# Bias tables copied within HBM and four temporaries of their own for six evictions in a transformer kernel on one Trainium2 core

## The chip, the core and the metric

The kernel runs on one core of one Trainium2 chip, as a single launch. The metric is the device time of one execution in microseconds. The times shown are those of three runs and of one execution that was taken with the hardware profiler. The engines are named as in the profile: PE (TensorE, with PEld for its weight loads), DVE (VectorE), ACT (ScalarE), POOL (GpSimd) and SP (SyncE, which here issues the weight DMAs).

## The reference

The input is one sequence of 512 tokens of width 1024 in float32. It goes through two layers of a first block and one layer of a second block. In outline (norms, gains and rotary embeddings are left out):

```
for l in 0, 1:
    x = x + 0.5 * swiglu(norm(x), ffn1_w_gu[l], ffn1_w_down[l])
    h = norm(x)
    parts of h @ w_in[l]:
        o_a = stick-breaking attention (4 heads)
        o_b = compressed + selected + windowed attention (8 heads, 2 key groups)
        o_c = attention over the 256 best keys by an indexer (4 heads)
    g_a, g_b, g_c = sigmoid(h @ w_gate[l])
    x = x + (g_a * (o_a @ w_br_a) + g_b * (o_b @ w_br_b) + g_c * (o_c @ w_br_c)) @ w_out
    x = x + 0.5 * swiglu(norm(x), ffn2_w_gu[l], ffn2_w_down[l])
second block:
    dilated attention in 3 groups of 8 heads, with a bias table per group and head,
    beside a gated convolution; then a swiglu FFN
```

The bias of the dilated attention depends on the distance of query and key and on the head alone: `bias_tab[rel_bucket(offset * dilation)]`.

## The kernel before

Activations lie transposed, 1024 channels in eight chunks of 128 partitions by 512 tokens. All weights come as one stream of 550 units of 128 x 1024 float32 (512 KB) in the order in which they are used. SP loads them into a ring of three staging buffers (`w_dma`, L133), ACT makes a rounded high part (L141) and DVE the rest (L142, `w_prep`), into a ring of five. A product is three matmuls, high x high, high x low and low x high (`mm3`, L172 to L174). The weights are prepared three units ahead of the unit in use.

The code is written as generators. A main generator yields after each product and holds the stream's matmuls; in the two mixers a side generator (`gen_side`: indexer, compression, attention) runs beside it. The side generator waits at named flags that the main one sets. A scheduler then orders the instructions of each engine by priority and by its own estimate of durations; each engine executes its list strictly in that order, waiting for what an instruction needs.

FFN front (`gen_ffn`): the norm's factor per token is not known when the first products run. The first two units, c = 0 and 1, are computed on unnormed input; then `stats_a` (L218, L223) and `rsqrt` (L205 to L210) make the factor, and `bcast` spreads it with a matmul (L231, L232, L233) into `rb`, which each eviction multiplies in (L261). The next units follow one by one up to c = 12.

Bias tables (`bias_rows`, L1005): in the very first FFN, after unit 2, three pairs of small matmuls (L1015) look up the bias rows of each group, DVE adds a mask (L1018), and POOL writes each group's 8 rows of 384 values 128 times into the HBM tensor `dr_b` (L1019), which the second block's attention reads much later (L1172), each partition from another offset:

```
t = self.f(o + 2328 + 384 * g, 384)[0:8]
nc.vector.tensor_tensor(t, ps[0:8, 0:384], cb[...], op=ALU.add)
nc.gpsimd.dma_start(self.dr_b[g], t[:, None, :].to_broadcast([8, 128, 384]))
```

Mixer front (`gen_mix`): after a first group for the indexer (`ev1`), the main generator computes two column blocks for the compressed keys and values (a "tunit" is one such block of eight products) and four for the stick-breaking queries and keys. Each is evicted from its PSUM bank by a multiplication with `rb` into a temporary (L470 in `ev_cmp`, L486 in `ev_sb`), which `split` (L179, L180, L182, L183) turns into two parts. There are two temporaries, in the region M_PT. The indexer (`gen_idx`) uses the same two as room for its transposed copies: `tpose_dup` copies to them (L592) and transposes them on PE (L595); its scores are L630, and DVE adds them up (L636). After the front the main generator goes on with the compression's first product (L500, L501), further column groups, 24 gate units (L522) and the first branch. M_NQ, 2048 values wide, later takes the queries of the sparse attention (`group(w["nq"])`).

The attention pairs of the side work are L777 (scores), L793 (transposes) and L801 (values).

Of the kernel before, what the change touches and what calls it, by code (L numbers as in the profile page):

```python
# [9 lines left out]
F32 = mybir.dt.float32  # L10
# [46 lines left out]
M_NQ = M_SV + 1024  # L57
M_SC = M_NQ + 2048
M_P = M_SC + 1152
M_PT = M_P + 2048  # L60
# [49 lines left out]
class Build:  # L110
# [133 lines left out]
    def gen_ffn(self, wgu, wdn, l, done, halves=None):  # L244
        nc = self.nc
        Y = A_Y
        gs = [self.f(Y + 1536 + 512 * i, 512) for i in range(2)]
        tt = [self.f(Y + 2560 + 512 * i, 512) for i in range(2)]
        rb = self.f(A_RB, 512)
        ring = tuple(range(8))  # L250

        def fs(c):
            o = R_O + (c % FSLOTS) * 1024
            return self.r(o, 512), self.r(o + 512, 512)

        def gkey(c, up, k):
            return (wgu, l, np.arange(128 * k, 128 * k + 128), np.arange(128) + 128 * c + up * DFF)

        def evac(c, pg, pu):
            i = c % 2  # L260
            nc.vector.tensor_tensor(gs[i], pg, rb, op=ALU.mult)  # L261
            nc.scalar.activation(gs[i], gs[i], AF.Silu)
            nc.vector.tensor_tensor(gs[i], pu, gs[i], op=ALU.mult)  # L263
            hi, lo = fs(c)
            self.split(hi, lo, gs[i])

        def up(cs):
            ps = {(c, up): self.bank(ring) for c in cs for up in (0, 1)}
            order = [(c, up, k) for c in cs for up in (0, 1) for k in range(8)]
            if len(cs) == 2:  # L270
                order.sort(key=lambda e: e[2])
            for c, up, k in order:
                self.mm3(ps[c, up], self.w(gkey(c, up, k)), self.h(k), k == 0, k == 7)
                yield
            if len(cs) == 2:
                pst = self.bank(ring)
                self.bcast(self.stats_a((self.acc,), pst), tt_flat, pst, rb)
            for c in cs:
                evac(c, ps[c, 0], ps[c, 1])
            if cs[0] == 2 and self.first:  # L280
                self.first = False
                self.bias_rows()

        tt_flat = self.f(Y + 2560, 512)

        def down(grp, cs):
            nk = len(cs)
            if grp == 0:
                order = [(m, j) for m in range(8) for j in range(nk)]
            else:  # L290
                order = [(m, j) for m in range(2) for j in range(nk - 1)] + [(m, nk - 1) for m in range(2)]
                order += [(m, j) for m in range(2, 6 if halves else 8) for j in range(nk)]
            ps = {}
            for m, j in order:
                if j == 0:
                    ps[m] = self.bank(ring)
                key = (wdn, l, np.arange(128) + 128 * cs[j], np.arange(128) + 128 * m)
                self.mm3(ps[m], self.w(key), fs(cs[j]), j == 0, j == nk - 1)
                yield
                if j == nk - 1:  # L300
                    done(grp, m, ps[m], tt[m % 2], rb)
            if grp == 0 or not halves:
                return

            tl = {}
            for i in range(2):
                sl = slice(256 * i, 256 * i + 256)
                for m in (6, 7):
                    ps = self.bank(ring)[:, sl]
                    for j in range(nk):  # L310
                        if i == 0:
                            tl[m, j] = self.w((wdn, l, np.arange(128) + 128 * cs[j], np.arange(128) + 128 * m))
                        self.mm3(ps, tl[m, j], [a[:, sl] for a in fs(cs[j])], j == 0, j == nk - 1)
                        yield
                    done(grp, m, ps, tt[m % 2][:, sl], rb, sl)
                halves(i)

        c0 = list(range(11))
        c1 = list(range(11, 22))
        for cs in [(0, 1)] + [(c,) for c in range(2, 13)]:  # L320
            yield from up(cs)
        yield from down(0, c0)
        for c in c1[2:]:
            yield from up((c,))
        yield from down(1, c1)
# [60 lines left out]
    def gen_mix(self, l):  # L386
        nc = self.nc
# [54 lines left out]
            with self.late(-5000):  # L442
                evac(ps)

        def tmp2(i, o=M_PT):
            return self.f(o + (i % 2) * 512, 512)

        def ev1(t, ps):
            for o, n, p in ((M_IQ + t * 288, 288, 0), (M_G1 + t * 160, 160, 288)):
                nc.scalar.activation(self.f(o, n), ps[:, p:p + n], AF.Copy, scale=rc[:, t:t + 1])  # L450
# [8 lines left out]
        def blk(kv, hl):  # L459
            return 1122 * (2 * kv + hl)  # L460
# [5 lines left out]

        def ev_cmp(kv):
            def evac(ps):
                t = tmp2(kv)
                nc.vector.tensor_tensor(t, ps, rb, op=ALU.mult)  # L470
                for g in range(2):
                    sl = slice(64 * g, 64 * g + 64)
                    o = 544 * g
                    self.split(stk[sl, blk(kv, 0) + o:blk(kv, 0) + o + 512],
                               stk[sl, blk(kv, 1) + o:blk(kv, 1) + o + 512], t[sl])
                b = stk[:, blk(kv, 0):blk(kv, 0) + 2244].rearrange("p (h n) -> p h n", h=2)
                nc.gpsimd.dma_start(b[64:128, :, 0:511], b[0:64, :, 1:512])
                nc.gpsimd.dma_start(b[0:64, :, 545:1057], b[64:128, :, 544:1056])
            return evac
# [2 lines left out]

        def ev_sb(i):
            def evac(ps):
                t = tmp2(i)
                nc.vector.tensor_tensor(t, ps, rb, op=ALU.mult)  # L486
                self.split(self.r(R_QK + i * 1024, 512), self.r(R_QK + i * 1024 + 512, 512), t,
                           scale=0.125 if i < 2 else None)
            return evac
# [3 lines left out]
        for kv in range(2):  # L493
            ps = self.bank(ring)
            o = ps[:, 0:192].rearrange("p (l g c) -> p l g c", l=2, c=32)
# [22 lines left out]
        for m in range(8):  # L518
            for br in range(3):
                def evac(ps):  # L520
                    t = tmp2(n, M_IQ)
                    nc.vector.tensor_tensor(t, ps, rb, op=ALU.mult)  # L522
                    nc.gpsimd.dma_start(self.dr_g[m, :, br * 512:br * 512 + 512], t)
                yield from tunit("w_gate", np.arange(128) + 1024 * br + 128 * m, evac)
                n += 1

        self.mt = self.h_tile(F32)
        for m in range(8):
            g = self.merged(m)
# [475 lines left out]
    def bias_rows(self):  # L1005

        nc = self.nc
        o = A_Y + 3584
        cb = self.f(o, 2304)[0:32]
        nc.scalar.dma_start(cb, self.ap["cb"])  # L1010
        tab = self.f(o + 2304, 24)[0:32]
        nc.scalar.dma_start(tab, self.ap["par"][2][0:32, 296:320])
        for g in range(3):
            ps = self.bank(tuple(range(8)))
            nc.tensor.matmul(ps[0:8, 0:384], lhsT=tab[:, 8 * g:8 * g + 8], rhs=cb[:, 384 * g:384 * g + 384],  # L1015
                             start=True, stop=True)
            t = self.f(o + 2328 + 384 * g, 384)[0:8]
            nc.vector.tensor_tensor(t, ps[0:8, 0:384], cb[0:8, 1152 + 384 * g:1536 + 384 * g], op=ALU.add)  # L1018
            nc.gpsimd.dma_start(self.dr_b[g], t[:, None, :].to_broadcast([8, 128, 384]))  # L1019

    def gen_mix2(self):
        nc = self.nc
# [402 lines left out]
    def run(self, upto=99, start=0):  # L1425
        tc, nc, ap = self.tc, self.nc, self.ap
        with tc.tile_pool(name="sb", bufs=1) as sb, tc.tile_pool(name="hp", bufs=1) as self.hp, \
# [9 lines left out]
            self.sqt = [self.f(A_Y + 512 + 512 * i, 512) for i in range(2)]  # L1437
            self.dr_x = dr.tile([128, 4096], F32, name="dr_x")
            self.dr_b = dr.tile([3, 8, 128, 384], F32, name="dr_b")
            self.dr_c = dr.tile([8, 128, 512], F32, name="dr_c")  # L1440
            self.dr_s = dr.tile([512, 12], F32, name="dr_s")
            self.m2 = {}
# [17 lines left out]
            for l in range(2 if start == 0 else 0):  # L1460
                g = par[:, 24 * l:24 * l + 24]
# [22 lines left out]
            o = M  # L1484
# [100 lines left out]
```

## Time and profile before

| | |
|---|---|
| median of 3 runs | 3531.94 us |
| the three runs | 3525.71, 3531.94, 3532.26 us |
| profiled execution, its own time | 3525.48 us |
| span of that execution, first to last instruction | 3523.7 us |
| mean granted TensorE clock | 0.985 of 2.4 GHz |
| busy: PE, DVE, ACT, POOL | 3423.5, 1998.7, 1316.1, 320.0 us |
| chain that ended last | PE 91%, DMA 3%, DVE 3% of the span |

Busy time is the time in which an engine had an instruction in execution. PE's matmuls overlap (a 128 x 512 one lasts 0.39 us and the next starts about 0.23 us later), so a stretch's work on PE is better read from the number of matmuls than from the busy share. The granted clock has two levels, 1.2 GHz (0.50) and 2.4 GHz (1.00); a mean between them is a mixture. Of a wait the profile names the instruction that ended it. "SPq" and "POOLq" are DMA issues.

### The profile page before, as it was taken

The page shows a single profiled execution, that of the slowest core. Times are in us where ns is not written, and L with a number is a line of the kernel's source. Part 1 is how long each engine was busy: PE and PEld are TensorE (multiplying, and loading weights), DVE is VectorE, ACT ScalarE, POOL GpSimd, SP SyncE. Part 2 cuts the span into 40 slices and gives each one's busy share as a digit, 9 for nine tenths or more (in the row PEclk, how much of TensorE's full clock was granted, in tenths as well). Part 3 has the DMA queues.
Part 4 walks back from the last instruction along what each step waited for, and adds up shares of the span by engine and source line. Part 5 has one row for each costly group of instructions (what it writes and reads, how often), then busy time and mean ns, then how long its engine had stood idle before and what let it go on. Part 6 is the DMA issues. An engine that isn't in the chain of part 4 may idle for free.

```text
span 3523.7 us, 43236 instructions
## 1 busy us (share of the span) xinstructions
PE 3423.5 (97%) x16884; PEld 2793.6 (79%) x16884; DVE 1998.7 (57%) x3733; ACT 1316.1 (37%) x2234; POOL 320.0 (9%) x355
## 2 busy tenths in 40 slices
PE   6899999999999999999999999999999999999997
PEld 5688888776888888888887768888877777878886
DVE  4344488566544444344886666443488998554344
ACT  3222354356332233223544464322344443443232
POOL 2000100010300010001000104000111112220002
PEclk8999999999999999999999999999999999999998
DMA  6722322331322222223322314223333224522221
GB/s 149 116 99 96 120 91 87 108 115 54 132 96 96 96 96 96 96 100 116 96 89 98 112 42 149 95 97 100 108 105 92 83 79 141 183 80 98 97 96 54
DMA packets 100814, 357.05 MB, mean 101 GB/s; under 512 B 14168, under 2 KB 16984, under 8 KB 99808
## 3 DMA queue, kind: packets, MB, share of 16 engines
q1 hardware_dynamic: 81504, 290.49, 24.6%
q0 software_dynamic: 18144, 61.76, 6.9%
q8 instruction: 132, 2.16, 0.3%
q10 hardware_dynamic: 960, 2.04, 0.2%
q14 instruction: 74, 0.61, 0.1%
HBM read 320.05 MB, written 32.08 MB: 100 GB/s over the span
## 4 chain that ended last, share of the span: by engine, by line
PE 91%; DMA 3%; DVE 3%; ACT 1%; issue 1%; POOL 0%; DVEq 0%; ACTq 0%; POOLq 0%
PE pb L172 27%; PE pb L173 27%; PE pb L174 27%; DMA af<-wst 2%; PE pb L801 2%; PE pb L793 1%; PE pb L777 1%; PE pb L1193 1%; PE pb L595 1%; PE pb L737 1%; PE pb L1290 1%; PE pb L1266 1%; PE pb L756 0%; DVE af L1351 0%; DVE ar L142 0%
## 5 line engine op out<-in xcount | busy, mean ns | idle before, releaser
L141 ACT ACTIVATE ar<-af 128x1024 fp32r<-128x1024 f32 x550 | 582.7, 1060 | 1517.5 <-PE pb L173 968.2
L172 PE MATMUL pb<-h,ar 128*128 128x512 f32 x2848 | 1114.2, 394 | 33.9 <-ACT ar L141 15.1
L174 PE MATMUL pb<-h,ar 128*128 128x512 f32 x2848 | 1120.1, 393 | 0.1
L173 PE MATMUL pb<-h,ar 128*128 128x512 f32 x2848 | 1119.4, 393 | 0.0
L142 DVE TENSOR_TENSOR ar<-af,ar 128x1024 fp32r<-128x1024 f32 x550 | 687.7, 1251 | 447.6 <-ACT ar L141 446.1
L172 PEld LDWEIGHTS pb<-h,ar 128*128 128x128 f32 x2848 | 538.0, 189 | 151.1 <-ACT h L239 16.2
L174 PEld LDWEIGHTS pb<-h,ar 128*128 128x128 f32 x2848 | 537.7, 189 | 114.6 <-issue 3.2
L173 PEld LDWEIGHTS pb<-h,ar 128*128 128x128 f32 x2848 | 537.9, 189 | 113.6 <-issue 3.2
L173 PE MATMUL pb<-ar 128*128 128x512 f32 (+1 forms) x1254 | 483.2, 386 | 1.2 <-DVE ar L183 1.2
L174 PE MATMUL pb<-ar 128*128 128x512 f32 (+1 forms) x1254 | 482.8, 386 | 0.0
L172 PE MATMUL pb<-ar 128*128 128x512 f32 (+1 forms) x1254 | 481.8, 386 | 0.6 <-DVE af L779 0.5
L172 PEld LDWEIGHTS pb<-ar 128*128 128x128 f32 x1254 | 235.6, 188 | 49.4 <-DVE af L779 1.2
L200 POOL TENSOR_TENSOR af<-af 128x512 f32<-128x512 f32 (+1 forms) x76 | 109.7, 1444 | 1816.5 <-ACT af L198 1805.5
L173 PEld LDWEIGHTS pb<-ar 128*128 128x128 f32 x1254 | 235.6, 188 | 49.0 <-DVE ar L183 2.4
L174 PEld LDWEIGHTS pb<-ar 128*128 128x128 f32 x1254 | 235.6, 188 | 47.1
L263 DVE TENSOR_TENSOR af<-pb,af 128x512 f32<-128x512 f32 x110 | 75.6, 690 | 299.0 <-PE pb L174 297.9
L261 DVE TENSOR_TENSOR af<-pb,af 128x512 f32<-128x512 f32 x110 | 75.5, 691 | 247.0 <-PE pb L174 231.9
L1132 DVE SCALAR_TENSOR_TENSOR af<-af 128x512 f32<-128x512 f32 x240 | 179.4, 748 | 3.6
L172 PE MATMUL pb<-ar,h 128*128 128x256 f32 (+1 forms) x448 | 133.4, 298 | 0.0
L173 PE MATMUL pb<-ar,h 128*128 128x256 f32 (+1 forms) x448 | 132.4, 296 | 0.0
L174 PE MATMUL pb<-ar,h 128*128 128x256 f32 (+1 forms) x448 | 132.0, 295 | 0.0
L180 DVE TENSOR_TENSOR ar<-af,ar 128x512 fp32r<-128x512 f32 (+4 forms) x178 | 114.3, 649 | 16.2 <-ACT ar L179 15.6
(236 smaller groups left out, 3185.3 us busy)
## 6 DMA issues: line engine op xcount, KB each, us to landing
af<-wst SPq DMA_DIRECT2D x550, 512.0 KB, 3.3
dr_g<-af POOLq DMA_DIRECT2D x64, 256.0 KB, 2.3
af<-dr_g POOLq DMA_DIRECT2D x24, 512.0 KB, 4.6
dr_x<-af POOLq DMA_DIRECT2D x3, 2048.0 KB, 7.5
af<-dr_x POOLq DMA_DIRECT2D x3, 2048.0 KB, 8.7
dr_b<-af POOLq DMA_DIRECT2D x3, 1536.0 KB, 63.3
h<-dr_g POOLq DMA_DIRECT2D x16, 256.0 KB, 5.5
af<-x POOLq DMA_DIRECT2D x8, 256.0 KB, 12.3
```

The source lines that it names most:

```text
L141: self.nc.scalar.activation(self.r(o, UNIT), st, AF.Copy)
L142: self.nc.vector.tensor_tensor(self.r(o + UNIT, UNIT), st, self.r(o, UNIT), op=ALU.subtract)
L172: mm(out, lhsT=w[0], rhs=a[0], start=start, stop=False, skip_group_check=True)
L173: mm(out, lhsT=w[0], rhs=a[1], start=False, stop=False, skip_group_check=True)
L174: mm(out, lhsT=w[1], rhs=a[0], start=False, stop=stop, skip_group_check=True)
L180: self.nc.vector.tensor_tensor(lo, src, hi, op=ALU.subtract)
L200: nc.gpsimd.tensor_tensor(acc, acc, t, op=ALU.add)
L261: nc.vector.tensor_tensor(gs[i], pg, rb, op=ALU.mult)
L263: nc.vector.tensor_tensor(gs[i], pu, gs[i], op=ALU.mult)
L595: self.nc.tensor.transpose(ps[:, 128 * i:128 * i + 128], t[:, 128 * i:128 * i + 128], self.f(A_C + C_ID, 128))
L801: first[u] = self.behind(first[u], mm(out[64 * u:64 * u + 64], lhsT=v[u][:, j, :], rhs=pts[u][:, 128 * j:128 * j + 128], start=first[u] is ...
L1132: nc.vector.scalar_tensor_tensor(a, u[:, j:j + 512], w[:, j:j + 1], a, op0=ALU.mult, op1=ALU.add)
```

## The change

Two things. The first FFN calls `bias_rows` after unit 8 instead of unit 2, and each table goes to HBM in two steps: the 8 rows once to a new HBM tensor `dr_r` (12 KB), and from there 128-fold to `dr_b`. The six evictions of the mixer's front no longer use the two temporaries at M_PT but four at M_NQ, the compressed keys and values the first two, the four others 2, 3, 0, 1. What else was written to `tmp2` (the gates, at M_IQ) stays. Lines after the additions are numbered 3 to 5 higher.

```diff
@@ gen_ffn, up
-            if cs[0] == 2 and self.first:
+            if cs[0] == 8 and self.first:
                 self.first = False
                 self.bias_rows()
@@ gen_mix
-        def tmp2(i, o=M_PT):
+        def tmp2(i, o):
             return self.f(o + (i % 2) * 512, 512)
+
+        def tmp4(i):
+            return self.f(M_NQ + (i % 4) * 512, 512)
@@ ev_cmp
-                t = tmp2(kv)
+                t = tmp4(kv)
@@ ev_sb
-                t = tmp2(i)
+                t = tmp4(2 + i)
@@ bias_rows
-            nc.gpsimd.dma_start(self.dr_b[g], t[:, None, :].to_broadcast([8, 128, 384]))
+            nc.gpsimd.dma_start(self.dr_r[g], t)
+            nc.gpsimd.dma_start(self.dr_b[g], self.dr_r[g][:, None, :].to_broadcast([8, 128, 384]))
@@ run
+            self.dr_r = dr.tile([3, 8, 384], F32, name="dr_r")
```

The order of instructions moves in two places. The first is POOL's queue in the first FFN, before (L200 adds up squares, the first ones while the input arrives, the last ones at the FFN's end):

```order
L200 ISA
L200 TENSOR_TENSOR af<-af 128x512 x5
L1019 DMA dr_b<-af 1024x1x384
L200 TENSOR_TENSOR af<-af 128x512 x2
L1019 DMA dr_b<-af 1024x1x384 x2
L200 TENSOR_TENSOR af<-af 128x512 x6
```

and after the change:

```order
L200 ISA
L200 TENSOR_TENSOR af<-af 128x512 x7
L1022 DMA dr_r<-af 8x384 x2
L1023 DMA dr_b<-dr_r 1024x1x384
L1022 DMA dr_r<-af 8x384
L1023 DMA dr_b<-dr_r 1024x1x384 x2
L200 TENSOR_TENSOR af<-af 128x512 x6
```

The first table no longer stands between the sums of squares of the input; all three stand behind them, each behind a store that it reads. On PE the bias matmuls stand behind unit 8.

The second place is PE in the front of mixer 1, where the second tunit of the main stream (bank pb_70) ends. Before (the indexer's transposes are L595, its scores L630):

```order
L172 MATMUL pb_70<-h,ar 128x512
L173 MATMUL pb_70<-h,ar 128x512
L174 MATMUL pb_70<-h,ar 128x512
L595 MATMUL pb_74<-af 128x128 x4
L595 MATMUL pb_75<-af 128x128 x4
L630 MATMUL pb_71<-ar 128x256
L630 MATMUL pb_72<-ar 128x256
L630 MATMUL pb_73<-ar 128x256
L595 MATMUL pb_74<-af 128x128
L595 MATMUL pb_75<-af 128x128 x4
```

and after the change:

```order
L172 MATMUL pb_70<-h,ar 128x512
L173 MATMUL pb_70<-h,ar 128x512
L174 MATMUL pb_70<-h,ar 128x512
L172 MATMUL pb_69<-h,ar 128x512
L173 MATMUL pb_69<-h,ar 128x512
L174 MATMUL pb_69<-h,ar 128x512
```

Before, 36 matmuls of the indexer stand in a row there (26 L595, 10 L630; 43 in mixer 2), and the third tunit, in bank pb_69, follows them. Now the third tunit follows at once, and the indexer's matmuls stand between the main ones further down.

## Rows read from the trace of the kernel before

**Rows 1.** Busy time by engine, from the page: us (share of the span) xinstructions.

```profile
PE 3423.5 (97%) x16884; PEld 2793.6 (79%) x16884; DVE 1998.7 (57%) x3733; ACT 1316.1 (37%) x2234; POOL 320.0 (9%) x355
```

**Rows 2.** Waits of PE, 0 to 230 us: who for whom, us, times, longest.

```profile
PE pb L232 <- DVE af L231: 18.6, 1, 18.6
PE pb L172 <- ACT ar L141: 15.1, 2, 10.5
```

**Rows 3.** Windows of the first FFN; columns: us, PE, PEld, DVE, ACT, POOL, PEclk, DMA, GB/s.

```profile
40.00:70.00 30.00, 11.40 (x40) 8.28 (x39) 8.76 (x22) 6.54 (x7) 0.00 (x0) 0.66 0.45 106
70.00:110.00 40.00, 40.00 (x174) 31.56 (x173) 12.34 (x17) 7.84 (x12) 2.14 (x2) 1.00 0.84 59
110.00:150.00 40.00, 24.87 (x85) 18.52 (x84) 12.64 (x16) 10.55 (x14) 0.00 (x0) 0.79 0.89 138
150.00:230.00 80.00, 80.00 (x355) 66.26 (x354) 34.43 (x40) 21.76 (x26) 0.00 (x0) 1.00 0.32 107
47.00:52.00 5.00, 0.00 (x0) 0.00 (x0) 0.84 (x1) 1.06 (x1) 0.00 (x0) 0.50 0.53 85
95.00:100.00 5.00, 5.00 (x24) 4.14 (x23) 0.00 (x0) 0.00 (x0) 0.00 (x0) 1.00 1.01 55
```

**Rows 4.** Timeline of POOL, the three table writes: start us, us, line, op.

```profile
22.33 1.11 POOL L1019 DMA_DIRECT2D dr_b<-af  x1
74.27 1.09 POOL L1019 DMA_DIRECT2D dr_b<-af  x1 [47.80 <-DVE af L1018]
77.06 1.05 POOL L1019 DMA_DIRECT2D dr_b<-af  x1 [1.70 <-DVE af L1018]
```

**Rows 5.** DMA issues, 20 to 72 us: count, KB each, median us to landing.

```profile
dr_b<-af POOLq DMA_DIRECT2D x1, 1536.0 KB, 35.6
```

**Rows 6.** DMA issues of the whole span, from the page.

```profile
af<-wst SPq DMA_DIRECT2D x550, 512.0 KB, 3.3
dr_x<-af POOLq DMA_DIRECT2D x3, 2048.0 KB, 7.5
af<-dr_x POOLq DMA_DIRECT2D x3, 2048.0 KB, 8.7
dr_b<-af POOLq DMA_DIRECT2D x3, 1536.0 KB, 63.3
```

**Rows 7.** Timeline of ACT and PE in the first FFN, where weights were late.

```profile
50.07 1.06 ACT L141 ACTIVATE ar<-af 128x1024 fp32r<-128x1024 f32 x1 [24.41 <-DMA af<-wst]
62.55 1.22 PE L232 MATMUL pb<-af 128*128 128x512 f32 x1 [18.60 <-DVE af L231]
123.30 0.80 PE L172 MATMUL pb<-h,ar 128*128 128x512 f32 x1 [10.50 <-ACT ar L141]
```

**Rows 8.** Timeline of PE, front of mixer 1: gap of the main stream.

```profile
455.54 1.17 PE L595 MATMUL pb<-af 128*128 128x128 f32 x8
468.38 0.79 PE L172 MATMUL pb<-h,ar 128*128 128x512 f32 x1 [0.20 <-DVE af L470]
```

**Rows 9.** Timeline of DVE, front of mixer 1: the first eviction.

```profile
466.57 0.69 DVE L470 TENSOR_TENSOR af<-pb,af 128x512 f32<-128x512 f32 x1 [0.22 <-PE pb L595]
```

**Rows 10.** Timeline of PE, front of mixer 2: the same gap.

```profile
1701.05 0.71 PE L595 MATMUL pb<-af 128*128 128x128 f32 x5
1717.63 0.50 PE L172 MATMUL pb<-h,ar 128*128 128x512 f32 x1 [1.65 <-DVE af L470]
```

**Rows 11.** Windows of the mixers: restarts, front, middle, tail; columns as in rows 3.

```profile
469.00:473.00 4.00, 4.00 (x11) 3.13 (x10) 3.81 (x9) 2.31 (x5) 0.62 (x1) 0.50 0.00 0
1718.00:1723.00 5.00, 5.00 (x16) 3.92 (x15) 4.84 (x11) 2.24 (x4) 0.62 (x1) 0.66 0.28 56
473.00:570.00 97.00, 96.44 (x704) 90.53 (x703) 90.73 (x249) 46.99 (x91) 2.31 (x5) 1.00 0.32 99
570.00:790.00 220.00, 219.87 (x1184) 172.80 (x1184) 142.71 (x372) 104.44 (x232) 17.34 (x32) 1.00 0.32 107
800.00:860.00 60.00, 53.04 (x410) 37.84 (x410) 42.90 (x149) 41.80 (x106) 0.59 (x1) 1.00 0.00 1
```

## The prediction

> **What bounds the kernel now.** I read the page's first section, then the waits, then the windows of the stretches in which TensorE waited. The matmul engine is busy for 97% of the span [rows 1], so time can be won only where it stands still, runs at its lower clock, or is given less to do. The change removes no matmul. So the question is which standstills it ends. Of the first 230 us the waits of PE name two of size beside the start itself [rows 2]: 18.6 us for the broadcast of the norm and 15.1 us for weight splits.
>
> The windows show what this costs. From 150 to 230 us PE issues 355 matmuls in 80 us, 4.44 a microsecond. From 40 to 150 us it issues 40 + 174 + 85 = 299, which take 67.4 us at that rate: **42.6 us are lost in this stretch** [rows 3], part of it at 0.66 and 0.79 of the clock, that is, partly at 1.2 GHz after the engine had stood still. What fills the stretch are the three bias tables: issued at 22.33, 74.27 and 77.06 us [rows 4], the first landing after 35.6 us [rows 5], the median of the three after 63.3, whereas a weight unit of 512 KB takes 3.3 us as a median of all 550 [rows 6]. From 70 to 110 us the DMA engines are 0.84 busy and move 59 GB/s, and from 150 on 0.32 busy for 107 GB/s [rows 3]. The tables hold the engines without moving much, and the weights behind them starve: at 123.30 us PE goes on after 10.50 us of waiting for a weight split, so it stopped at 112.8 us [rows 7].
>
> **Part one, the bias rows.** Three pairs of bias matmuls, three small additions and three table writes move from behind unit 2 of the first FFN to behind unit 8, six units of 48 matmuls further down, some 65 us of PE's work. Each table is now written in two steps: a 12 KB store, and a copy within HBM. The stores add three DMAs to POOL's queue. POOL has no work behind them but the sums of squares at the end of the FFN, and the tables are read in the last stage only, so waiting for them costs nothing.
>
> What goes: the two standstills with their slow restarts, 42.6 us. What stays of it: the two bias pairs inside the stretch (70 to 110 us has 174 matmuls where 177.5 fit, 0.8 us) and the two passes of the broadcast itself (about 1 us, 0.6 more than two ordinary matmuls). That leaves **41.2 us**. The norm's small DVE operations were queued behind weight splits, and one of these waited 24.41 us for its unit, until 50.07 us [rows 7], with the first table in flight; at 3.3 us a unit it could have started by about 30 us, well before PE asked for the broadcast (62.55 - 18.60 = 43.95 us [rows 7]), so nothing else is late there.
>
> What comes: the copies, at a place where the weights run ahead. How far ahead is measured by the second jam: PE went on from 74.27 to 112.8 us, **38.5 us of cover**. The trace has no copy within HBM. Nearest are a store and a load of 2048 KB, 7.5 and 8.7 us [rows 6]; for 1536 KB that makes 5.6 and 6.5 us. The ends are then 5.6 us a table (the write alone) and 35.6 us (no better than from SBUF [rows 5]), for three 17 to 107 us. I take 6.5 us, since a DMA reads and writes at once, so 20 us for three; even reading and writing in turn gives 36 us. Both lie inside the cover, so I cost the copies at nothing; beyond the cover each microsecond costs 0.76 (the second jam ended at 77.06 + 63.3 = 140.4; from 112.8 that is 27.6 us, and 40 - 85/4.44 = 20.9 us were lost). Why nearer to the load than to the old table: the store of 2048 KB from 128 partitions shows that writing to HBM isn't what made the table slow; its source in eight partitions is what remains, and that source goes.
>
> [...]
>
> **Part two, the six evictions.** In mixer 1 the main stream's second tunit ends at 455.54 us, and its next matmul begins at 468.38 us, having waited for L470 [rows 8]. L470 itself waited for a transpose, L595 [rows 9]: its temporary at M_PT is also the indexer's. In mixer 2 the same gap runs from 1701.05 to 1717.63 us [rows 10]. In the order after the change the next tunit follows at once, and the indexer's matmuls stand between main matmuls, so the change does what it says. Gain in mixer 1: 12.84 us less the 36 indexer matmuls in the gap, which must still run, at 1.17/8 = 0.15 us [rows 8], 5.3 us, so 7.5; and the slow restart, 11 matmuls in 4 us where 17.8 fit [rows 11], 1.5. Sum 9.0 us. Mixer 2: 16.58 less 43 times 0.15 is 10.3, plus 1.4 for 16 matmuls in 5 us where 22.2 fit: 11.7 us.
>
> Against it stands the mixer's tail. After the change 404 matmuls of the side work follow the last one of the main stream in both mixers; before there were 346 and 322. The tail keeps PE 53.04 of 60 us busy over 410 matmuls [rows 11], so each of 140 more costs 0.017 us of standing still, 2.4 us. DVE is short too: between 473 and 570 us it has 6.3 us free, and mixer 1 wants to be 9.0 us shorter; 2.7 us a mixer would be missing if nothing could be put off, but from 570 to 790 us DVE has 77 us free [rows 11], and the indexer's selection rounds can wait. I count 20.7 - 2.4 = **18.3 us**. The ends are 0 (the side work sets the mixer's end) and 26 (its matmuls cost half of 0.15 us, pipelined).
>
> **Sum.** 3525.5 (the profiled execution's own time; its span is 3523.7) - 41.2 - 18.3 = 3466.0 us. That execution equals the fastest of the three runs, and the median is 6.5 us above it; the runs stand in two groups, so I put the forecast half way between, **3469 us**.
>
> **Rivals.** *Half the engines.* With one table in flight the DMA share is 0.53, with two 1.01 [rows 3]: a table seems to occupy half of the engines, and its eight rows still stand outermost. At half the rate three tables take 39 us one behind the other, no loss; if reading and writing also take turns, 73 us, and (73 - 38.5) x 0.76 = 26 us are lost: 3470 to 3495 us. Against it: three copies in flight can fill both halves. Chance 0.15. [...]
>
> *The side work ends the mixer.* The main stream gets ahead of a chain (scores, attention pairs, tail) that isn't faster, and the gap comes back as a longer tail. For it: the first attention pair stands behind 49 and 95 more main matmuls than before. Against it: PE is busy 219.87 of 220 us from 570 to 790 [rows 11], so that chain waits for PE, not for itself. Then only part one counts: 3487 us. Chance 0.15.
>
> *Slower: the copies hold the engines for longer than the old tables.* Every copy reads the same 1536 bytes 128 times over; if one place in HBM serves that slowly, the jam returns at unit 8 with three tables in it. It eats the whole gain of 59.5 us when it lasts 38.5 + 59.5/0.76 = 117 us, that is, below 40 GB/s for 4.72 MB; the old table alone made 44 GB/s. At 30 GB/s it lasts 157 us and costs 90: 3559 us. Chance 0.04.
>
> *Both parts disappoint,* the copies by some 15 us and the mixers by all: about 3502 us. Chance 0.04.
>
> **Numbers.** My forecast has 0.62. The range 3451 to 3500 us holds it with the upper end of part two, the half of the engines, and the side work; outside are the two last cases and the edges, under 0.2. A change of less than 0.2%, 7 us, can't be told from none. Faster needs only that the jam be shorter than about 107 us: 0.95; within 0.2%: 0.02; slower: 0.03.
>
> **What would show it.** Right: no wait of PE for L232 or L141 in the first 230 us beyond 2 us, and 4.4 matmuls a microsecond from 10 to 400 us; the copies landing within 38 us; no gap in the main stream behind the second tunit of either mixer; the mixers' ends 9 and 11 us nearer to their starts. Wrong: weight units landing after 20 us or more behind unit 8, with PE waiting for L141 there; in the mixers, PE waiting for DVE between the second tunit and the compression, or a tail without main matmuls that is longer by as much as the front is shorter.

## The result and the profile after

The changed kernel takes **3467.4 us** (median of four runs, 3465.7 to 3468.4), the kernel before, run beside it, 3532.0 us (3525.7 to 3532.3). The ratio is 0.9821, with a 95% interval from 0.9804 to 0.9838: 1.8% faster. The forecast was 3469 us, within 3451 to 3500.

The span of the profiled execution went from 3523.7 to 3465.3 us, by 58.4. PE's busy time, against [rows 1]:

```profile
PE 3406.9 (98%) x16884; PEld 2784.8 (80%) x16884; DVE 1999.1 (58%) x3733; ACT 1314.8 (38%) x2234; POOL 322.3 (9%) x358
```

The matmuls are the same 16884; PE stands still for 58.4 us instead of 100.2, and the same matmuls keep it busy for 16.6 us less, the granted clock's mean having risen from 0.985 to 0.993: fewer of them run slowly behind a standstill. Where this happened is read from three points that both programs pass: the first matmul of each mixer (L172, 128x448) and the first addition of its product to x (L998 before, L1001 after). Timelines of PE and DVE, of the kernel before:

```profile
416.70 0.36 PE L172 MATMUL pb<-ar,h 128*128 128x448 f32 x1
909.95 1.28 DVE L998 TENSOR_TENSOR af<-af,pb 128x512 f32<-128x512 f32 x2
1662.83 0.36 PE L172 MATMUL pb<-ar,h 128*128 128x448 f32 x1
2158.73 1.28 DVE L998 TENSOR_TENSOR af<-af,pb 128x512 f32<-128x512 f32 x2
```

and of the changed one:

```profile
375.15 0.36 PE L172 MATMUL pb<-ar,h 128*128 128x448 f32 x1
858.83 1.28 DVE L1001 TENSOR_TENSOR af<-af,pb 128x512 f32<-128x512 f32 x2
1611.70 0.36 PE L172 MATMUL pb<-ar,h 128*128 128x448 f32 x1
2098.48 1.28 DVE L1001 TENSOR_TENSOR af<-af,pb 128x512 f32<-128x512 f32 x2
```

Up to mixer 1: 41.55 us less. Mixer 1: 493.25 and 483.68, 9.57 less. Between the mixers: the same. Mixer 2: 495.90 and 486.78, 9.12 less. From there to the end: 1.85 us more (last section). The sum is the 58.4.

**First FFN.** Windows of the changed kernel, columns as in [rows 3]:

```profile
40.00:70.00 30.00, 30.00 (x132) 24.48 (x131) 15.72 (x20) 13.92 (x18) 0.00 (x0) 1.00 0.27 88
70.00:110.00 40.00, 40.00 (x178) 33.10 (x178) 16.40 (x19) 11.15 (x14) 0.00 (x0) 1.00 0.26 93
110.00:150.00 40.00, 40.00 (x174) 31.62 (x173) 17.18 (x21) 11.16 (x14) 4.87 (x6) 1.00 0.60 211
```

Where 299 matmuls ran in these 110 us there are 484 now, and the granted clock is 1.00 in all three windows. Of PE's waits in the first 230 us one is left, that for the input, which stood before as well:

```profile
PE pb L172 <- ACT h L239: 9.1, 1, 9.1
```

POOL's timeline shows the stores (L1022) and copies (L1023); the second fence gives the time from issue to landing of the three copies, and of the weight units issued from 112 to 150 us:

```profile
115.73 1.11 POOL L1023 DMA_DIRECT2D dr_b<-dr_r  x1
116.84 0.50 POOL L1022 DMA_DIRECT2D dr_r<-af  x1
118.38 1.10 POOL L1023 DMA_DIRECT2D dr_b<-dr_r  x1 [1.04 <-DMA dr_r<-af]
128.68 1.08 POOL L1023 DMA_DIRECT2D dr_b<-dr_r  x1 [9.20 <-DMA dr_r<-af]
```

```profile
DMA to landing us min/median/max: 12.3/14.1/14.1
DMA to landing us min/median/max: 3.3/5.4/7.7
```

A copy takes 12 to 14 us, the set 27 us (115.73 to about 142.8), and a weight unit among them at most 7.7 us, where it was up to 49.9 us among the old tables. The third copy starts late because its 12 KB store, issued right behind the first copy (116.84 us), took 11.6 us to land; nothing else waits for it.

**Mixers.** Each mixer as one window, before and after (the second mixer shows the same: 11.97 and 7.64 us of standstill for 2856 matmuls):

```profile
416.70:909.95 493.25, 480.14 (x2847) 390.80 (x2846) 352.91 (x900) 249.95 (x523) 55.57 (x66) 0.99 0.30 101
```

```profile
375.15:858.83 483.68, 474.20 (x2847) 386.65 (x2846) 353.93 (x901) 250.74 (x523) 55.93 (x66) 1.00 0.30 103
```

For the same 2847 matmuls PE stands still for 9.5 us instead of 13.1 and is busy for 5.9 us less: the indexer's matmuls now run among the main ones, and the slow restart behind the gap of [rows 8, 11] is gone (the granted clock is 1.00 from 395 to 520 us). In the front of mixer 1, from 395 to 520 us, the profile has no wait of PE at all, in that of mixer 2, from 1612 to 1760 us, one of 0.2 us. Of the gain, 1.0 us is given back in the last 128 us of mixer 1 (standstill 8.2 before, 9.2 after) and 0.4 us in mixer 2 (6.0 and 6.4).

### The profile page after: what moved, and what is told of

Read it like the earlier page. It is cut to its first block, busy times and chain, and to the rows that moved or that the text cites. A ratio compares the mean times of both kernels' runs of the same rounds, so it can differ in the third digit from the quotient of the medians.

```text
span 3465.3 us, 43214 instructions
## 1 busy us (share of the span) xinstructions
PE 3406.9 (98%) x16884; PEld 2784.8 (80%) x16884; DVE 1999.1 (58%) x3733; ACT 1314.8 (38%) x2234; POOL 322.3 (9%) x358
## 4 chain that ended last, share of the span: by engine, by line
PE 92%; issue 3%; DVE 2%; DMA 1%; ACT 1%; POOL 0%; DVEq 0%; POOLq 0%; ACTq 0%
PE pb L172 28%; PE pb L173 28%; PE pb L174 28%; PE pb L804 1%; PE pb L1197 1%; PE pb L796 1%; PE pb L780 1%; PE pb L740 1%; PE pb L598 1%; PE pb L1294 1%; PE pb L1270 1%; PE pb L759 0%; DVE af L1355 0%; DMA af<-dr_g 0%; PE pb L754 0%
## 5 line engine op out<-in xcount | busy, mean ns | idle before, releaser
L141 ACT ACTIVATE ar<-af 128x1024 fp32r<-128x1024 f32 x550 | 582.8, 1060 | 1479.2 <-PE pb L173 987.2
L172 PE MATMUL pb<-h,ar 128*128 128x512 f32 x2848 | 1112.2, 393 | 16.9 <-ACT h L239 13.1
L172 PEld LDWEIGHTS pb<-h,ar 128*128 128x128 f32 x2848 | 536.9, 189 | 132.3 <-ACT h L239 15.5
L172 PE MATMUL pb<-ar 128*128 128x512 f32 (+1 forms) x1254 | 481.4, 386 | 0.8 <-DVE af L782 0.5
L172 PEld LDWEIGHTS pb<-ar 128*128 128x128 f32 x1254 | 235.6, 188 | 49.7 <-DVE af L782 1.2
L200 POOL TENSOR_TENSOR af<-af 128x512 f32<-128x512 f32 (+1 forms) x76 | 110.0, 1448 | 1723.4 <-ACT af L198 1712.2
L172 PE MATMUL pb<-ar,h 128*128 128x256 f32 (+1 forms) x448 | 132.9, 297 | 0.2 <-ACT af L431 0.2
L180 DVE TENSOR_TENSOR ar<-af,ar 128x512 fp32r<-128x512 f32 (+5 forms) x178 | 114.4, 649 | 11.2 <-ACT ar L179 10.5
## 6 DMA issues: line engine op xcount, KB each, us to landing
dr_b<-dr_r POOLq DMA_DIRECT2D x3, 1536.0 KB, 14.1
```

The lines of the kernel that those rows point to most:

```text
L141: self.nc.scalar.activation(self.r(o, UNIT), st, AF.Copy)
L172: mm(out, lhsT=w[0], rhs=a[0], start=start, stop=False, skip_group_check=True)
L180: self.nc.vector.tensor_tensor(lo, src, hi, op=ALU.subtract)
L200: nc.gpsimd.tensor_tensor(acc, acc, t, op=ALU.add)
```

## The experiments

All are compared with the kernel before on the same chip; as its median lay between 3527 and 3532 us in the four sets, ratios say more than differences.

### The two parts apart

`x3_temps_only` is the kernel before with the four temporaries, `x4_tables_only` the changed kernel without them:

```diff
# x4_tables_only, against the changed kernel (x3_temps_only: only these two lines are changed)
-                t = tmp4(kv)
+                t = tmp2(kv, M_PT)
-                t = tmp4(2 + i)
+                t = tmp2(i, M_PT)
```

Expected of x3_temps_only: 

> The kernel before with the four temporaries alone; tables as before. Theory (the two parts add up, and the mixers gain what the traces show, 9.6 and 9.1 us): 3513 us against 3532, the stretch before mixer 1 as long as before (416.7 us). Rival (the mixers' gain depends on what the first part left, or the second block gives it back): 3525 us or more.

Expected of x4_tables_only: 

> The changed kernel with the two temporaries at M_PT as before; tables as changed. Theory (parts add up; first mixer begins 41.5 us earlier, the gap behind the second tunit is there as before): 3490 us against 3532. Rival: below 3480 or above 3500 us, the gain of one part being tied to the other.

Measured: 3508.8 us for the temporaries (ratio 0.9947, 0.9932 to 0.9961; 18.3 us) and 3483.5 us for the tables (0.9873, 0.9857 to 0.9890; 43.5 us). The product of the ratios is 0.9821, that of the change: the parts add up, and neither lives on the other.

### Place or form of the tables

```diff
# x1_move_only: behind unit 8, written from SBUF as before
-            nc.gpsimd.dma_start(self.dr_r[g], t)
-            nc.gpsimd.dma_start(self.dr_b[g], self.dr_r[g][:, None, :].to_broadcast([8, 128, 384]))
+            nc.gpsimd.dma_start(self.dr_b[g], t[:, None, :].to_broadcast([8, 128, 384]))
# x2_copy_at_unit2: store and copy as in the change, behind unit 2
-            if cs[0] == 8 and self.first:
+            if cs[0] == 2 and self.first:
```

Expected of x1_move_only: 

> The changed kernel, but each table is written 128-fold straight from its eight SBUF partitions, as before, now behind unit 8. Theory (the source in eight partitions makes the jam, the place alone doesn't help): the first table took 35.6 us alone and the other two 63.3 us together, so three issued within 5 us take about 99 us; the weights run 38.5 us ahead, and each microsecond beyond costs 0.76: 46 us more than the change's 3467.4, about 3513 us, with PE waiting for L141 twice or more behind unit 8 and weight units landing after 40 us or more. Rival (unit 2 was only a bad place, the weights running ahead at unit 8 cover it): 3467 to 3472 us and no wait of PE for L141.

Expected of x2_copy_at_unit2: 

> The changed kernel, but the bias rows stay behind unit 2, with the store and the copy within HBM. Theory (the form is what counts): the copies land in some 14 us each as in the changed kernel, the weights among them are late by under 5 us, and the time is 3467 to 3473 us. Rival (the place counts too: with one copy in flight from 22 us on, the weight splits and so the norm's broadcast are late again): PE waits 10 to 20 us for L231 at L232, 3478 to 3488 us.

The copy behind unit 2 takes 3467.4 us (0.9830, 0.9816 to 0.9845), the changed kernel's time to 0.1 us, with no wait of PE but that for the input, weight units landing after 9.8 us at most and the copies after 12.5 to 16.0. **With the copy, the place is worth nothing.** The move alone takes 3493.5 us (0.9903, 0.9889 to 0.9918), 26 us above the change. PE's waits for weight splits in its first 380 us, five windows, and the landings of its tables and of the weight units among them (112 to 220 us):

```profile
PE pb L172 <- ACT ar L141: 19.3, 3, 7.1
```

```profile
120.00:140.00 20.00, 20.00 (x90) 16.57 (x89) 4.63 (x6) 3.52 (x6) 0.00 (x0) 1.00 0.98 64
160.00:180.00 20.00, 8.97 (x27) 6.07 (x28) 4.03 (x5) 3.15 (x4) 0.00 (x0) 0.70 1.01 94
140.00:220.00 80.00, 60.58 (x232) 46.97 (x231) 17.88 (x21) 12.59 (x16) 0.00 (x0) 0.85 0.79 106
150.00:180.00 30.00, 16.52 (x61) 11.98 (x60) 4.03 (x5) 3.15 (x4) 0.00 (x0) 0.80 1.01 92
180.00:220.00 40.00, 34.06 (x128) 26.70 (x128) 12.02 (x15) 8.86 (x10) 0.00 (x0) 0.85 0.59 126
```

```profile
DMA to landing us min/median/max: 67.4/70.8/101.1
DMA to landing us min/median/max: 3.2/24.2/50.1
```

Three tables take 101 us, as expected (99), and units up to 50 us. From 140 to 220 us 232 matmuls run where 355 would, which is 27.7 us, the distance by which mixer 1 begins later than after the change (402.78 against 375.15). The expected loss was 46 us, from a cover of 38.5 us and 0.76 a microsecond beyond it. PE first stopped 44 us after the first issue, at 157.6 us. Up to 180 us it lost 16.2 us, 0.72 a microsecond; from 180 to 220 us, with two of the three tables landed or about to (after 67 and 71 us), 11.2 us in 40. So the price held while several tables were in flight and was too high for the last one.

### Does a jam beyond the cover cost?

```diff
# x6_nine_copies: two more copies of each table, to a tensor that nothing reads
             nc.gpsimd.dma_start(self.dr_b[g], self.dr_r[g][:, None, :].to_broadcast([8, 128, 384]))
+            for e in range(2):
+                nc.gpsimd.dma_start(self.dr_d[2 * g + e], self.dr_r[g][:, None, :].to_broadcast([8, 128, 384]))
```

Expected: 

> The changed kernel with every table copied three times within HBM (twice more to a spare HBM tensor), nine copies behind unit 8. Three copies took 27 us from the first issue to the last landing. Theory (any jam longer than the cover is paid for): nine take about 81 us; beyond a cover of 38.5 to 44 us each microsecond costs 0.48 to 0.76, 18 to 32 us, so 3485 to 3500 us. Rival (a copy, unlike a table from SBUF, lets the weights through: units landed after 5.4 us as a median and 7.7 us at most among the three copies, and PE needs one every 5.4 us): 3467 to 3472 us, no wait of PE for L141, units landing within 10 us however long it lasts.

Measured: 3466.4 us (0.9822, 0.9807 to 0.9837), no wait for L141. The theory falls. One window of it beside the same window of `x1_move_only`, and the weight units' landings (112 to 195 us):

```profile
120.00:170.00 50.00, 50.00 (x222) 41.42 (x221) 19.48 (x22) 12.95 (x17) 6.28 (x6) 1.00 0.99 309
```

```profile
120.00:170.00 50.00, 42.89 (x182) 34.63 (x181) 8.88 (x11) 5.67 (x8) 0.00 (x0) 0.93 0.99 75
```

```profile
DMA to landing us min/median/max: 3.2/9.8/15.8
```

The DMA engines are busy to 0.99 in both. Among the copies they move 309 GB/s, and units land after 9.8 us (16 at most); among the old tables 75 GB/s and 24.2 us (50 at most). The copies are in flight for some 70 us, nearly twice the cover, and cost nothing; of the rival's forecast only the 10 us for a unit didn't hold. **Here the busy share doesn't tell whether weights starve; how late they land, against the lead that they have, does.**

### One old table at a time

```diff
# x9_spaced: the old write, one table behind each of the units 4, 8 and 12
-            if cs[0] == 8 and self.first:
-                self.first = False
-                self.bias_rows()
+            if cs[0] in (4, 8, 12) and self.first:
+                self.first = cs[0] < 12
+                self.bias_rows(cs[0] // 4 - 1)
```

Expected: 

> The changed kernel with the old tables from eight partitions, one behind each of the units 4, 8 and 12, some 43 us apart. Theory (the old form hurts only where the jam outlasts the cover of 38.5 to 44 us; one table alone takes 35.6): the tables land in some 36 us, one after the other, PE doesn't wait, 3467 to 3473 us. Rival (one table in flight starves the weights as well, and between two there is no time to get ahead again): PE waits for L141 behind units 8 and 12, 3478 to 3495 us.

Measured: 3467.7 us (0.9828, 0.9812 to 0.9845), PE without a wait. The tables' landings, the weight units' (69 to 195 us), a window, and the queues in the same window (q0 has the table, q1 the weights: packets, MB, share of 16 engines):

```profile
DMA to landing us min/median/max: 35.9/36.1/37.3
DMA to landing us min/median/max: 3.1/14.8/23.5
```

```profile
120.00:150.00 30.00, 30.00 (x134) 24.86 (x133) 10.05 (x12) 6.35 (x8) 0.00 (x0) 1.00 0.62 114
```

```profile
q0 software_dynamic: 303, 1.39, 41.8%
q1 hardware_dynamic: 551, 2.03, 20.0%
```

With one table in flight the weights come at 68 GB/s (2.03 MB in 30 us; the rest of the 114 GB/s is the table itself), less than the 107 of an undisturbed stretch [rows 3], and some units land late; but a table has landed before the cover is used up, and some 8 us lie between two tables. So the old form alone doesn't lose the 41 us either. It lost time here in two cases: with several tables in flight at once, and with a single one where the weights aren't ahead. The second case is the first jam of the kernel before. Its first table was alone in flight from 22.33 us on, for 35.6 us [rows 4, 5]. The weight units issued there from 20 to 60 us landed hardly later than in `x9_spaced`:

```profile
DMA to landing us min/median/max: 3.2/15.0/27.7
```

Yet PE waited for the norm's broadcast, and from 40 to 70 us 40 matmuls ran where 133 fit: 21 of the 42.6 us lost [rows 3, 7].

### What makes a table slow

```diff
# x7_outer128: the 128 repetitions outermost in the copy
-            nc.gpsimd.dma_start(self.dr_b[g], self.dr_r[g][:, None, :].to_broadcast([8, 128, 384]))
+            nc.gpsimd.dma_start(self.dr_b[g].rearrange("h c n -> c h n"), self.dr_r[g][None].to_broadcast([128, 8, 384]))
# x8_src128_unit2: behind unit 2, t holds each row on 16 partitions, and each writes it 8 times
+            nc.gpsimd.dma_start(self.dr_b[g].rearrange("h (j c) n -> (h j) c n", c=8), t[:, None, :].to_broadcast([128, 8, 384]))
```

Expected of x7_outer128: 

> The changed kernel, with the copy written so that its outermost dimension is the 128 repetitions and the eight rows lie inside. Theory (eight rows outermost keep the copy to half of the 16 DMA engines): the last of the copies, alone in flight, lands after about 7 us where 14.1 were seen, the DMA share meanwhile near 1 where it was 0.8, and the whole set is done in some 15 to 20 us where it took 27; the time stays at 3467 +- 4 us, the copies being hidden already. Rival (a copy within HBM takes 14 us whatever its order, each byte being read and written): the same landings as in the changed kernel, the same time.

Expected of x8_src128_unit2: 

> The changed kernel without the copy within HBM and without the move: behind unit 2 the rows are looked up into 128 partitions (each row 16 times), and every partition writes its row eight times to the table. Theory (the old table was slow because its source lay in eight partitions): a table lands in 5 to 9 us, nothing waits, 3467 +- 4 us, for which neither the move nor the copy is needed. Rival (what was slow is writing 1024 pieces of 1536 bytes 128-fold from SBUF): a table takes 30 us or more, the waits for L231 and L141 come back, 3500 to 3510 us.

Measured: 3468.4 us (0.9827, 0.9813 to 0.9842) and 3472.4 us (0.9839, 0.9825 to 0.9854). The landings of the copies of `x7_outer128`; a window of it with two copies in flight for most of the time and one with a single copy; the same of the changed kernel; and the landings of the tables of `x8_src128_unit2`:

```profile
DMA to landing us min/median/max: 9.5/11.2/11.4
```

```profile
125.00:130.00 5.00, 5.00 (x24) 4.14 (x23) 2.31 (x3) 1.17 (x2) 0.29 (x1) 1.00 1.02 345
130.00:135.00 5.00, 5.00 (x24) 4.14 (x23) 1.41 (x3) 1.14 (x3) 0.00 (x0) 1.00 0.93 332
```

```profile
125.00:130.00 5.00, 5.00 (x24) 4.15 (x23) 2.52 (x3) 1.54 (x2) 1.08 (x1) 1.00 0.87 294
135.00:140.00 5.00, 5.00 (x24) 4.14 (x23) 2.52 (x3) 1.60 (x2) 0.00 (x0) 1.00 0.68 249
```

```profile
DMA to landing us min/median/max: 6.9/7.9/8.4
```

With the repetitions outermost the set takes some 20 us instead of 27 and the engines are busy to 0.93 and more from 115 to 135 us: the copy with eight rows outermost left them idle for a part of the time, most clearly with a single copy (0.68 against 0.93). With two in flight, from 120 to 125 us, a share of 0.99 moved no more than one of 0.86 (321 and 328 GB/s). The 7 us of the theory weren't reached, but no copy of this run was alone in flight for all of its time. From 128 partitions the same 1536 KB land in 8 us, and without a copy. That write differs from the old one in two things, the partitions of its source and its outermost dimension, 128 for eight. The copies price the second: with eight rows outermost they landed after 12.3 to 16.0 us (here and in `x2_copy_at_unit2`), with 128 after 9.5 to 11.4. So it is the source that made the table slow: 36 us from eight partitions, 8 us from 128, same bytes, same destination. The run is some 5 us slower than the change and just above the theory's range; 2.6 of these are the lookup's twelve wider matmuls (three groups of 1.6 us, where six narrow ones take 2.10 us), and the rest is open. In the profiled execution another 2.8 us lie in mixer 2 (489.6 us against 486.8), which varies by as much between runs with the same evictions.

### Which evictions, and how many temporaries

```diff
# y1_cmp_own: only the first two apart from the indexer
-                t = tmp4(2 + i)
+                t = tmp2(i, M_PT)
# y2_sb_own: only the four others
-                t = tmp4(kv)
+                t = tmp2(kv, M_PT)
# x5_two_temps: all six, on two
-                t = tmp4(kv)
+                t = tmp2(kv, M_NQ)
-                t = tmp4(2 + i)
+                t = tmp2(i, M_NQ)
```

Expected of y1_cmp_own: 

> The changed kernel, but only the first two evictions of the mixer's front (compressed keys and values) have temporaries of their own; the four of the stick-breaking queries and keys use the two at M_PT again, beside the indexer. Theory (every eviction that shares with the indexer ties the main stream to it): a row of some 33 indexer matmuls stands behind the third tunit instead of the second, the gap of 12 us and the restart come back one tunit later, and 14 to 18 of the 18.3 us of part two are lost: 3481 to 3486 us. Rival (only the first two matter, since the indexer is past its hand-over by then): 3466 to 3470 us.

Expected of y2_sb_own: 

> The changed kernel, but the first two evictions use the two temporaries at M_PT again and the four others have their own. Theory (as in the run beside it): the second eviction waits for the indexer, the gap stands one tunit further down than before, and most of the 18.3 us is lost: 3479 to 3486 us. Rival (four free ones are enough for the main stream to run on around the two): 3466 to 3472 us.

Expected of x5_two_temps: 

> The changed kernel with two temporaries of their own at M_NQ instead of four. The order of instructions on every engine is the same as in the changed kernel. Theory (what counts is that the indexer isn't in them; a temporary is free again after an eviction and its split, some 3 us, and the next tunit ends 5.5 us later): 3467 +- 3 us. Rival (four are needed, the evictions being late in DVE's queue): PE waits for an eviction in the front, 3470 to 3476 us.

Measured: 3483.8 us (0.9867, 0.9850 to 0.9885), 3488.7 us (0.9885, 0.9869 to 0.9901) and 3466.2 us (0.9818, 0.9801 to 0.9836). Without any of the six apart it was 3483.5. So a separation of some is worth nothing. In either run the main stream stops again for a row of indexer matmuls, now behind the third tunit: in mixer 1 for 9.4 us in `y1_cmp_own` and 11.8 in `y2_sb_own`, from 420 us on. `y2_sb_own` lies above the range expected; why it is the slower one is open. A window of the first mixer of `y1_cmp_own` shows the row (PE stands still for 2.74 us, and the granted clock is 0.83 in the mean); `x5_two_temps` in the same stretch runs through:

```profile
415.00:435.00 20.00, 17.26 (x78) 13.89 (x77) 16.78 (x37) 9.61 (x22) 0.58 (x1) 0.83 0.22 66
```

```profile
415.00:435.00 20.00, 20.00 (x109) 17.22 (x108) 16.20 (x32) 10.61 (x22) 0.58 (x1) 1.00 0.28 93
```

Two temporaries do as well as four; it is the region, not the number.

## Why the prediction was right, point by point

**Bias rows, 41.2 us.** The stretch up to mixer 1 became 41.55 us shorter, and the windows show 4.4 matmuls a microsecond from 40 us on (484 in 110 us), as the steps on what goes and what stays of it had it.

**What the copies cost.** Nothing, as forecast, but two steps to it were wrong. The price of 6.5 us a copy was half of what it is, 12.3 to 14.1 us; the set took 27 us, not 20. The step that chose the nearest rows took a store and a load from 128 partitions as the measure; a copy with eight rows outermost keeps the engines less busy, as the rival "half the engines" had it. That rival holds in part: a single copy in flight had a DMA share of 0.68 and 249 GB/s, against 0.93 and 332 with 128 outermost, but the landing became shorter by about a fifth and not by half. Its price didn't fall due. That a DMA reads and writes at once, the reason given for 6.5 us, was the author's estimate: the copies of `x7_outer128` landed after less time than the prices of store and load make in turn (9.5 to 11.4 us against 5.6 + 6.5 = 12.1), those with eight rows outermost after more. How many engines a copy had is not shown: the profiles give the share of all of them together.

**The cover.** The step "beyond the cover each microsecond costs 0.76" was carried over from the old tables to the copies, and there it fails: nine copies over 70 us cost nothing. With the copies the weights weren't starved (units landed after 7.7 us at most among three, after 15.8 among nine), so there was nothing to cover, and the place behind unit 8 isn't needed: the zero in the sum came true for another reason than the one given. The rival "slower" was priced by that step too; what it would take for copies to starve the weights no run shows. For old tables 0.76 held for the pair from which it was read, and gave 46 us where 27.6 were measured for three.

**Its source, not the writing.** The step that excluded the writing as the cause holds (36 us from eight partitions, 8 us from 128). Four tables from eight partitions, none beside another, took 35.6 to 37.3 us (the first of the kernel before, the three of `x9_spaced`); what in such a source makes them slow, no run shows.

**Mixers, 18.3 us.** The traces show 9.57 + 9.12 = 18.7 us, the run with the temporaries alone 18.3. By mixer the forecast was 9.0 and 11.7, less 1.2 for each tail. The first came out 1.8 us better than that, the second 1.4 us worse, which is no more than scatter: in the eight other profiled executions with all six evictions apart, mixer 1 took 483.1 to 486.7 us and mixer 2 484.4 to 489.6. The tails gave back 1.0 and 0.4 us. The rival that the side work ends the mixer so holds for 1.4 us of some 20.

**The whole.** 3466.0 us was the sum for the execution that was profiled; it took 3467.1. The difference is the 1.85 us behind the second mixer, which no step had, less what the parts brought beyond their estimates. The forecast of 3469 added 3 us, half of the distance between two groups of runs of the kernel before. Its 20 later runs lie spread from 3522.6 to 3534.0 us, so the two groups were an accident of three runs; the changed kernel's four lie within 2.7 us.

## What to carry to other kernels

A large DMA beside a weight stream is judged by how late the weights land and how far they run ahead, not by the busy share of the engines: at 0.99 busy, copies that moved 309 GB/s let a unit through in 10 us, tables from eight partitions at 75 GB/s in 24. A DMA whose source lies in few partitions, here eight, is to be spread over 128 or put through HBM first (36 us became 8, and 12 to 16, for the same 1536 KB). If neither is possible, it is issued one at a time and where the weights run ahead: one table alone cost nothing behind units 4, 8 and 12, and some 21 us behind unit 2. And two streams of work that share a temporary can be tied at each of its uses: separating some of the uses brought nothing here, all of them 18 us.

## What the runs showed that was not expected

The small store among the copies was late with them: 12 KB landed after 1.7 us alone, and after 11.6 us when issued right behind a copy, about when that copy landed.

The 1.85 us behind the second mixer are a matter of the clock. At the second block's front PE stands still for a moment in both kernels, then goes on. Windows around this point, before and after:

```profile
2566.25:2568.25 2.00, 0.80 (x2) 0.00 (x0) 1.11 (x1) 1.43 (x2) 0.00 (x0) 1.00 0.01 4
2570.25:2572.25 2.00, 2.00 (x10) 1.65 (x9) 2.00 (x4) 0.96 (x2) 0.00 (x0) 1.00 0.35 135
2572.25:2574.25 2.00, 2.00 (x11) 1.65 (x10) 0.10 (x1) 0.00 (x0) 0.00 (x0) 1.00 0.00 0
```

```profile
2506.00:2508.00 2.00, 0.79 (x2) 0.00 (x0) 1.12 (x1) 1.42 (x2) 0.00 (x0) 1.00 0.00 0
2510.00:2512.00 2.00, 2.00 (x7) 1.54 (x6) 2.00 (x4) 0.95 (x2) 0.00 (x0) 0.56 0.41 156
2512.00:2514.00 2.00, 2.00 (x7) 1.56 (x6) 0.08 (x1) 0.00 (x0) 0.00 (x0) 0.58 0.00 0
```

The same standstill of 1.2 us within a window, the same matmuls: once the granted clock stays at 1.00, once it goes down and back within 4 us (0.50 in the two windows of 1 us from 2511 to 2513 us), which costs 7 matmuls or 1.6 us. From 2500 to 2600 us its mean is 0.98 in `x6_nine_copies`, `x7_outer128` and `x9_spaced` and 1.00 in `x8_src128_unit2`, with the same standstill of 1.97 us in all four, so the change isn't what decides it; why it falls in one and not in the other, no run here tells. No trace gives the clock in GHz: the profile has it as a share of full speed. Differences of 2 us between two kernels with such standstills are not read as an effect of an edit.
